# The second MLP product of an encoder block in another order of its column halves, with 48 of 64 units by seven products in place of 42

## The chip, the cores and the metric

The kernel runs on one core of one Trainium2 chip. The metric is the device time of one execution in microseconds (us), taken as the median of several runs. The engines are named as in the profile: PE is TensorE (matmul), PEld its weight load, DVE is VectorE, ACT is ScalarE, POOL is GpSimd, SP is SyncE, which issues the loads.

## The reference

One layer of an encoder: x is 256 tokens by 2048 features, in float32. Two kinds of attention with a joint output projection, a cross attention to 256 memory tokens, and an MLP, each followed by a layer norm over the residual sum.

```python
def squared_relu_mlp(h, w_mlp_in, w_mlp_out):
    return jnp.square(jax.nn.relu(h @ w_mlp_in)) @ w_mlp_out
...
        x = layer_norm(ALPHA * x + xa, ln2_g[l], ln2_b[l])

        ff = squared_relu_mlp(x, w_mlp_in[l], w_mlp_out[l])
        x = layer_norm(ALPHA * x + ff, ln3_g[l], ln3_b[l])
```

The hidden layer is 8192 wide: w_mlp_in is 2048 x 8192 and w_mlp_out 8192 x 2048. The change concerns `h @ w_mlp_out` alone.

## The kernel before, in words

**Three matmuls for one product.** Each float32 operand is split into a high half (ACT copies it to the type fp32r) and a low half (DVE subtracts the high one from the source). `mm3` (lines 163 to 166) then issues high x high, high x low and low x high: three matmuls, 128 x 128 by 128 x 512 at most. The second is the first to need the low half of the weights. ACT works ahead of DVE, and both ahead of PE, as far as four buffers for high halves (`wsp`) and four for low halves (`fixed`) let them.

**The hidden layer** has 64 tiles of 128 columns, in four chunks c of 16 (`CH`, `NCH`). One tile (`hidden_tile`, line 1021) takes a 1 MB load of w_mlp_in in two parts of 1024 columns, each split, and issues 32 matmuls: 16 of 512 columns and 16 of 256. The tile is then evacuated by one small ACT and one small DVE operation (`evacuate`, lines 870 and 871). Two tiles make a pair p. A pair passes through `stages` (line 877): relu and square on ACT (883, 884), the split into halves (874, 875), and, for a pair that a seven-product unit will use, three additions on DVE (894 to 898) and one more split. The eight tiles of the first half chunk (`LEAD`) are made ahead of the passes, in two groups (`hidden_group`).

**The second product** goes in passes (c, q): chunk c by column half q (1024 of 2048 columns), eight passes in all, numbered 0 to 7 here. A pass has eight units, one for each pair. One unit is a 2 x 2 by 2 x 2 block product: two blocks of tokens, two tiles of the pair, two groups of 512 columns, and one 1 MB load of w_mlp_out.

- A *plain* unit makes eight block products, 24 matmuls; its weights come in two parts of 1024 columns to split.
- A *seven* makes seven block products (Strassen's scheme), 21 matmuls. It needs sums of the pair's tiles (above) and sums of the weights, which DVE adds into `s_t` (`push_sums`, line 942: one addition of 1024 columns and two of 512). Its weights come in four parts: 1024 and 512 from the load, 1024 and 1024 from `s_t`.

Before, units 0 to 5 of a pass are sevens and units 6 and 7 plain, and pass 7 has eight plain units: 42 sevens and 22 plain units. Pairs 0 to 5 of each chunk get sums.

**Banks.** The eight accumulators of PSUM are four for x11, x12, x21, x22 (`xs`) and four for the products p1, p5, p6, p7 (`pt`). At the end of each pass but the last DVE merges them into the residual `res`: four additions for `xs` and eight, called `banks`, for `pt` (lines 1105 to 1111 and 1147 to 1150), behind one ACT copy of p1. The eight are taken up one or two at a time, behind the splits that follow. A hidden tile borrows x22 among the sevens, and p1 and p6 in turn elsewhere.

**The order of the work.** `items` (lines 908 to 916) is the list of tiles (g) and units (u): about one tile ahead of each unit, so that the tiles of the next half chunk are made beside the units of this one; pass 7 has none. `fetch` issues the loads on SP, three to four items ahead, into a ring of buffers that `row_b` joins at the item `JOIN`. `part` (line 958) makes one split, counts it, and behind it issues what is due: deferred work (`after(n, ...)` means n parts from now), one merge, one weight addition. `queue` fixes the order of the instructions given to it, on each engine, as they are written; other instructions (the stages of most pairs, the merges) are placed by a scheduler. The stages of tile 15's pair are queued and are written behind the unit that follows the tile (`late_finish`). Hidden pairs lie in nine slots: eight in `ht`, one in `aux`, whose other seven places hold sums. A slot is given back behind the second pass of its chunk.

**Around the passes.** The residual also needs the gain and bias of the second layer norm, in two halves of 1024 features (`norm_ops`, line 1206): four DVE operations each on `row_b`. The first half goes beside the hidden groups, the second is put into pass 1 by `after(6 * i + 8, x)`. In the last pass the last four units (`HELD`) make the products of the first block of tokens as their weights come (12 matmuls each) and keep the split weights; those of the second block follow in the end, so that the last layer norm of the first block lies beside them.

## Time and profile before

| | before |
|---|---|
| median of 3 runs | 1100.84 us (1099.25 to 1100.96) |
| profiled execution, its own time | 1098.48 us |
| span of that execution | 1096.7 us |
| PE busy | 1077.8 us, 98% of the span |
| DVE busy | 937.5 us, 85% |
| ACT busy | 638.7 us, 58% |
| granted clock of TensorE | 0.997 |

A row of a timeline has the start, the duration, the engine, the line, the operation, output and inputs and the count; in brackets stands how long the engine idled before it and who released it. The page models the ends of matmuls, so a busy PE is not PE at its peak: whether it waited is read from the distance between starts, in the same kind of work. DVE's durations overlap the next start by some 0.08 us, so costs on DVE are also read from start to start. "att" and "acc" are the two groups of four accumulators.

### The profile page before, as it was taken

Reading aid. Unit: us, or ns where it says so; the run is one execution under the profiler, and the core shown is the slowest. Engines: PE = TensorE matmul, PEld = TensorE weight load, DVE = VectorE, ACT = ScalarE, POOL = GpSimd, SP = SyncE. Lnnn points to the kernel's source line nnn. Section 1 sums busy time; section 2 is a strip of 40 time slices with the busy share of each in tenths; the row PEclk is TensorE's granted clock in tenths of the full one; section 3 lists DMA queues with packets and bytes.
Section 4 is the critical chain, followed back from the end, with each engine's and each line's share of the span. In section 5 each row is a group of like instructions: output and inputs, shape, how many; then the busy total and the mean of one; then the engine's idle time right before and its main releaser. Section 6 shows DMA issues by size and latency. Waiting matters only on the chain.

```text
span 1096.7 us, 15276 instructions
## 1 busy us (share of the span) xinstructions
PE 1077.8 (98%) x5864; PEld 931.1 (85%) x5864; DVE 937.5 (85%) x1299; ACT 638.7 (58%) x925; POOL 35.6 (3%) x45
## 2 busy tenths in 40 slices
PE   9999999999999999999999999999999999999996
PEld 6988899988999878878888888888888888888885
DVE  6878677678879677999999999899999899999876
ACT  6555566546576426656567557466566566666640
POOL 2402000000100000000000000000000000000000
PEclk9999999999999999999999999999999999999998
DMA  9663453466576444555556555646556555645732
GB/s 330 242 226 138 153 193 136 160 244 221 185 224 240 151 149 174 212 192 194 193 198 242 210 179 209 213 171 228 195 189 223 200 192 195 226 171 194 254 149 78
DMA packets 37369, 215.87 MB, mean 197 GB/s; under 512 B 4272, under 2 KB 5168, under 8 KB 13616
## 3 DMA queue, kind: packets, MB, share of 16 engines
q1 hardware_dynamic: 37296, 214.89, 55.1%
q8 instruction: 46, 0.75, 0.3%
q14 instruction: 27, 0.22, 0.1%
HBM read 212.78 MB, written 2.10 MB: 196 GB/s over the span
## 4 chain that ended last, share of the span: by engine, by line
PE 92%; DVE 6%; issue 1%; ACT 1%; DMA 0%; POOL 0%; DVEq 0%; SPq 0%; ACTq 0%
PE acc L164 12%; PE acc L165 12%; PE acc L166 12%; PE acc L1029 11%; PE att L1029 6%; PE acc L1037 6%; PE att L165 5%; PE att L166 5%; PE att L164 5%; PE att L1037 3%; PE acc L206 2%; PE acc L204 2%; PE acc L205 2%; DVE lo L956 2%; PE acc L213 1%; PE att L213 1%
## 5 line engine op out<-in xcount | busy, mean ns | idle before, releaser
L88 DVE TENSOR_TENSOR w_lo<-raw,w_hi 128x1024 fp32r<-128x1024 f32 (+2 forms) x130 | 147.4, 1142 | 60.2 <-ACT w_hi L87 59.2
L87 ACT ACTIVATE w_hi<-raw 128x1024 fp32r<-128x1024 f32 (+2 forms) x134 | 131.6, 989 | 113.9 <-PE acc L166 68.3
L956 DVE TENSOR_TENSOR lo<-raw,w_hi 128x1024 fp32r<-128x1024 f32 (+1 forms) x156 | 173.0, 1127 | 9.2 <-ACT w_hi L955 9.0
L955 ACT ACTIVATE w_hi<-raw 128x1024 fp32r<-128x1024 f32 (+1 forms) x156 | 149.3, 980 | 25.7 <-PE acc L166 15.4
L1029 PE MATMUL acc<-x2t,w_hi 128*128 128x512 f32 x592 | 153.4, 391 | 0.0
L1029 PEld LDWEIGHTS acc<-x2t,w_hi 128*128 128x128 f32 x592 | 108.9, 189 | 19.6
L956 DVE TENSOR_TENSOR lo<-s_t,w_hi 128x1024 fp32r<-128x1024 f32 x84 | 102.4, 1222 | 10.8 <-ACT w_hi L955 10.8
L955 ACT ACTIVATE w_hi<-s_t 128x1024 fp32r<-128x1024 f32 x84 | 88.6, 1057 | 37.3 <-PE acc L1029 17.1
L1037 PEld LDWEIGHTS acc<-x2t,lo 128*128 128x128 f32 x592 | 80.8, 190 | 5.8
L1037 PE MATMUL acc<-x2t,lo 128*128 128x256 f32 x592 | 82.5, 282 | 0.0
L1029 PE MATMUL att<-x2t,w_hi 128*128 128x512 f32 x304 | 78.4, 391 | 0.0
L165 PE MATMUL acc<-lo,ht 128*128 128x512 f32 (+1 forms) x188 | 73.0, 389 | 1.1 <-DVE lo L956 1.1
L164 PE MATMUL acc<-w_hi,ht 128*128 128x512 f32 x186 | 72.5, 390 | 0.0
L166 PE MATMUL acc<-w_hi,ht 128*128 128x512 f32 x186 | 72.5, 390 | 0.0
L166 PE MATMUL acc<-w_hi,xt 128*128 128x512 f32 (+2 forms) x192 | 69.6, 364 | 0.0
L165 PE MATMUL acc<-w_lo,xt 128*128 128x512 f32 (+2 forms) x192 | 69.5, 363 | 0.0
L870 ACT ACTIVATE tmp<-acc 128x256 f32<-128x256 f32 x41 | 15.4, 384 | 92.2 <-PE acc L1029 87.9
L164 PE MATMUL acc<-w_hi,xt 128*128 128x512 f32 (+2 forms) x192 | 66.4, 366 | 0.7 <-ACT w_hi L87 0.7
L1029 PEld LDWEIGHTS att<-x2t,w_hi 128*128 128x128 f32 x304 | 55.8, 189 | 10.0
L165 PE MATMUL att<-lo,aux 128*128 128x512 f32 x139 | 54.4, 392 | 1.4 <-DVE lo L956 1.4
L956 DVE TENSOR_TENSOR lo<-raw_x,w_hi 128x1024 fp32r<-128x1024 f32 (+1 forms) x50 | 55.4, 1124 | 0.3 <-ACT w_hi L955 0.2
L164 PE MATMUL att<-w_hi,aux 128*128 128x512 f32 x139 | 54.1, 390 | 0.0
(293 smaller groups left out, 2519.0 us busy)
## 6 DMA issues: line engine op xcount, KB each, us to landing
raw<-in_w_mo SPq DMA_DIRECT2D x39, 1024.0 KB, 4.8
raw<-in_w_mc SPq DMA_DIRECT2D x37, 1024.0 KB, 4.8
raw<-in_w_out SPq DMA_DIRECT2D x16, 1024.0 KB, 4.9
raw_x<-in_w_mo SPq DMA_DIRECT2D x14, 1024.0 KB, 4.9
raw_x<-in_w_mc SPq DMA_DIRECT2D x12, 1024.0 KB, 4.8
row_b<-in_w_mo SPq DMA_DIRECT2D x11, 1024.0 KB, 4.8
raw<-in_w_mi SPq DMA_DIRECT2D x8, 1024.0 KB, 4.9
row_b<-in_w_mc SPq DMA_DIRECT2D x7, 1024.0 KB, 4.7
```

The costliest lines, as they stand in the source:

```text
L87: pin(nc.scalar.activation(hi, src, AF.Copy), pinned)
L88: return pin(nc.vector.tensor_tensor(out=lo, in0=src, in1=f(hi), op=ALU.subtract), pinned)
L164: keep(nc.tensor.matmul(ps, ah, bh, start=start, stop=False))
L165: keep(nc.tensor.matmul(ps, ah, bl, start=False, stop=False))
L166: keep(nc.tensor.matmul(ps, al, bh, start=False, stop=stop))
L204: nc.tensor.matmul(ps, hi, xt[:, k, 0:S], start=k == 0, stop=False)
L205: nc.tensor.matmul(ps, hi, xt[:, k, S:2 * S], start=False, stop=False)
L206: nc.tensor.matmul(ps, lo, xt[:, k, 0:S], start=False, stop=k == nk - 1)
L955: queue(nc.scalar.activation(hi, src, AF.Copy))
L956: queue(nc.vector.tensor_tensor(out=lo, in0=src, in1=f(hi), op=ALU.subtract))
L1029: queue(nc.tensor.matmul(ps, hi[:, k * P:(k + 1) * P], x2t[:, k0 + k, :], start=k0 + k == 0, stop=k0 + k == KT - 1))
L1037: queue(nc.tensor.matmul(ps[:, 0:S], lo[:, k * P:(k + 1) * P], x2t[:, k0 + k, 0:S], start=False, stop=False))
```

## The change

1. *Order.* The passes go (0,0), (0,1), (1,1), (1,0), (2,0), (2,1), (3,1), (3,0): column halves 0, 1, 1, 0. Where two passes in a row have the same half (1-2, 3-4, 5-6) they make one run, and the banks are merged at its end only. Pass 0 and pass 7 are runs of their own.
2. *Units.* `UNITS` and `ORDERS` write out each pass: P for plain, S for seven. There are 48 S and 16 P. The plain units stand at the ends of runs; pass 0 ends with an S, and pass 7 goes P S P S and then the four held plain units.
3. *Tiles.* `TILES` writes out how many tiles stand ahead of each unit. Passes 0, 2, 4 and 6 have none ahead of their last unit.
4. *Sums.* The pairs that get sums are those of `SUMS`: six, seven, seven and six of the four chunks, 26 in place of 24. Pairs 0 and 1 of chunk 0 have none.
5. *Slots.* Hidden pairs have eight slots and sums eight.
6. *Banks.* x22 is merged by itself behind the plain units that open a run, since tiles borrow it after that. `tile_bank` chooses the bank of each tile. The eight merges of `pt` come in another order.
7. *Row operations.* The second half of `norm_ops` goes into pass 0, at parts 6, 8, 10 and 12. `JOIN` becomes unit 4 of pass 0. The first evacuation in pass 0 is deferred by three parts, not four.

```diff
-    SEVEN = (0, 1, 2, 3, 4, 5)
-    PASSES = [(c, q) for c in range(NCH) for q in range(2)]
-    ORDER = tuple(range(CH // 2))
-    SEVENS = {cq: SEVEN for cq in PASSES[:-1]}
-    SEVENS[PASSES[-1]] = ()
     HELD = 4
     LEAD = CH // 2
-    SLOTS = CH // 2 + 1
+    PASSES = [(c, (n + c) % 2) for c in range(NCH) for n in range(2)]
+    UNITS = ["PPSSSSSS", "PPSSSSSS", "SSSSSSSP", "PSSSSSSS", "SSSSSSSP", "PSSSSSSS", "SSSSSSPP", "PSPSPPPP"]
+    ORDERS = [(0, 1, 2, 3, 4, 5, 6, 7), (0, 1, 2, 3, 4, 5, 6, 7), (0, 1, 2, 3, 4, 5, 6, 7), (7, 0, 1, 2, 3, 4, 5, 6),
+              (0, 1, 2, 3, 4, 5, 6, 7), (7, 0, 1, 2, 3, 4, 5, 6), (0, 1, 2, 3, 4, 5, 6, 7), (7, 0, 6, 1, 2, 3, 4, 5)]
+    TILES = ["21111110", "21111111", "11111110", "21111111", "11111110", "21111111", "11111110", "00000000"]
+    SEVENS = {cq: [p for p, x in zip(o, u) if x == "S"] for cq, o, u in zip(PASSES, ORDERS, UNITS)}
+    SUMS = [set(SEVENS[c, 0] + SEVENS[c, 1]) for c in range(NCH)]
...
-    place, free = {}, {"h": list(range(SLOTS)), "s": list(range(len(SEVEN) + 1))}
+    place, free = {}, {"h": list(range(CH // 2)), "s": list(range(len(sums_h)))}
...
-        return [square, halve] + [add, halve_sums] * (p in SEVEN)
+        return [square, halve] + [add, halve_sums] * (p in SUMS[c])
...
+    tiles = [("g", c, j) for c in range(NCH) for j in range(CH)][LEAD:]
+    for (c, q), order, counts in zip(PASSES, ORDERS, TILES):
+        for p, n in zip(order, counts):
+            items += [tiles.pop(0) for _ in range(int(n))] + [("u", c, q, p)]
+    JOIN = items.index(("u", 0, 0, 4))
...
-            after(4, lambda: evacuate(ps, h, j % 2, queue))
+            after(3 if j == LEAD else 4, lambda: evacuate(ps, h, j % 2, queue))
...
+        opens = n == 0 or PASSES[n - 1][1] != q
+        closes = final or PASSES[n + 1][1] != q
...
+        def tile_bank(it):
+
+            before, later_ = items[:at[0] - 1], items[at[0]:]
+            units = [x for x in before if x[0] == "u"][-1:] + [x for x in later_ if x[0] == "u"][:1]
+            if all(is_seven(x) for x in units) or it[1:] == (0, LEAD):
+                return x22
+            ahead = later_[:next(i for i, x in enumerate(later_) if is_seven(x))]
+            return p1 if sum(x[0] == "g" for x in ahead) % 2 or n == len(PASSES) - 2 else p6
...
-                if n_seven == len(sevens):
+                if run["s"] == 0:
                     nc.scalar.activation(m_t, p1, AF.Copy)
+                    xs_done = [lambda r=r, ps=ps: merge(r, ps) for r, ps in ((r12, x12), (r11, x11), (r21, x21))]
+                    banks.extend([lambda: merge(r11, m_t), lambda: more(p6)] + xs_done * (units[-1] == "S") + [
+                        lambda: merge(r22, p5), lambda: merge(r12, p5),
+                        lambda: merge(r12, m_t, ALU.subtract), lambda: more(p7, ALU.subtract),
+                        lambda: merge(r21, m_t), lambda: merge(r22, m_t, ALU.subtract)])
...
+                if not final and n_unit < len(units) and units[n_unit] == "S":
+                    banks.append(lambda: merge(r22, x22))
...
-            side.extend(wait * 4 + empty + [a1, b1, a3, a2, a4, b3] + both(b2, rows[0])
-                        + both(b4, rows[1]) + rows[2:])
+            (a1, a2), (b1, b2) = first, second
+            side.extend(wait * 4 + empty + [a1, b1, a2, b2] + rows)
...
-    for cq in PASSES:
-        if cq == (0, 1):
-            for i, x in enumerate(norm_ops(1)):
-                after(6 * i + 8, x)
-        one_pass(*cq)
+    for i, x in enumerate(norm_ops(1)):
+        after(2 * i + 6, x)
+    for n in range(len(PASSES)):
+        one_pass(n)
```

## The prediction, made before the changed kernel ran

> **What bounds the kernel now.** I read the page first, then the busy time in chosen stretches, then the timelines of single engines. The page:

> ```profile
> span 1096.7 us, 15276 instructions
> PE 1077.8 (98%) x5864; PEld 931.1 (85%) x5864; DVE 937.5 (85%) x1299; ACT 638.7 (58%) x925; POOL 35.6 (3%) x45
> DVE  6878677678879677999999999899999899999876
> PE 92%; DVE 6%; issue 1%; ACT 1%; DMA 0%; POOL 0%; DVEq 0%; SPq 0%; ACTq 0%
> ```

> TensorE carries 92% of the chain that ended last. VectorE carries 6%, but from the middle of the span on it is over 90% busy: a second engine close behind the first. So I cut the MLP at the starts of hidden tiles; one stretch is a tile and the unit behind it (columns: length, then busy time of PE, PEld, DVE, ACT, POOL, then clock, DMA, GB/s).

> ```profile
> 462.53:474.04 11.51, 10.95 (x54) 8.70 (x53) 11.41 (x17) 8.21 (x12) 0.00 (x0) 1.00 0.49 169
> 474.04:485.29 11.25, 10.64 (x55) 8.78 (x53) 11.15 (x16) 6.57 (x10) 0.00 (x0) 1.00 0.54 201
> 485.29:498.03 12.74, 10.91 (x55) 8.70 (x53) 11.57 (x16) 8.92 (x12) 0.00 (x0) 1.00 0.48 166
> 498.03:508.37 10.34, 10.34 (x54) 8.86 (x53) 9.43 (x11) 6.27 (x9) 0.00 (x0) 1.00 0.57 203
> 555.88:566.70 10.82, 10.70 (x54) 8.77 (x53) 10.82 (x16) 7.49 (x11) 0.00 (x0) 1.00 0.56 194
> 566.70:577.63 10.93, 10.62 (x54) 8.78 (x53) 10.90 (x13) 6.43 (x9) 0.00 (x0) 1.00 0.56 189
> 577.63:588.91 11.28, 10.67 (x55) 8.73 (x53) 11.28 (x16) 7.48 (x11) 0.00 (x0) 1.00 0.74 269
> 599.25:610.28 11.03, 11.03 (x57) 9.42 (x56) 11.03 (x16) 6.46 (x9) 0.00 (x0) 1.00 0.65 211
> 894.40:904.75 10.35, 10.35 (x55) 8.86 (x53) 10.35 (x16) 7.33 (x10) 0.00 (x0) 1.00 0.58 204
> 904.75:915.09 10.34, 10.34 (x54) 8.86 (x53) 10.01 (x12) 6.34 (x9) 0.00 (x0) 1.00 0.57 204
> ```

> A tile with a seven-product unit takes 10.345 us where nothing waits, a tile with a plain unit 11.03 us. In six stretches, three in pass 0 and three in pass 1, it takes longer, and there DVE is busy nearly throughout. Over 10.345 us they lose 1.165 + 0.905 + 2.395 = 4.465 us in pass 0 and 0.475 + 0.585 + 0.935 = 1.995 us in pass 1: 6.46 us. One such wait, in PE's timeline:

> ```profile
> 493.68 0.50 PE L165 MATMUL acc<-lo,ht 128*128 128x512 f32 x1 [1.06 <-DVE lo L956]
> ```

> The second matmul of a group needs the low half of the weights, which DVE makes last. So the MLP is bound by TensorE's issue, except where DVE has more than 10.345 us to do in a stretch.

> **TensorE's part.** Plain minus seven is 11.03 - 10.345 = 0.685 us, three matmuls of 0.228 us. Six more sevens (42 to 48, by the strings: 6+6+7+7+7+7+6+2) remove 18 matmuls: **-4.1 us**, all on the path. The number of tiles stays. [...]

> **VectorE's part.** One cycle without a wait:

> ```profile
> 904.69 1.22 DVE L948 TENSOR_TENSOR s_t<-raw 128x1024 f32<-128x1024 f32 x1
> 905.82 1.22 DVE L956 TENSOR_TENSOR lo<-row_b,w_hi 128x1024 fp32r<-128x1024 f32 x1
> 906.96 1.41 DVE L948 TENSOR_TENSOR s_t<-s_t,raw 128x512 f32<-128x512 f32 x2
> 908.28 1.82 DVE L956 TENSOR_TENSOR lo<-raw,w_hi 128x1024 fp32r<-128x1024 f32 x2
> 910.02 1.22 DVE L956 TENSOR_TENSOR lo<-s_t,w_hi 128x1024 fp32r<-128x1024 f32 x1
> 911.16 0.42 DVE L871 TENSOR_TENSOR tmp<-acc,tmp 128x256 f32<-128x256 f32 x1
> 911.88 1.23 DVE L956 TENSOR_TENSOR lo<-s_t,w_hi 128x1024 fp32r<-128x1024 f32 x1 [0.30 <-ACT w_hi L955]
> 913.02 1.22 DVE L956 TENSOR_TENSOR lo<-raw_x,w_hi 128x1024 fp32r<-128x1024 f32 x1
> ```

> From start to start a 1024-column operation costs 1.135 us, a 512-column one 0.60 (1.74 - 1.135), two dependent adds 1.32, an evacuation about 0.36. Tile and seven: 6 x 1.135 + 0.60 + 1.32 + 0.36 = 9.1 us. Every second tile also closes a pair:

> ```profile
> 455.51 0.42 DVE L894 TENSOR_TENSOR tmp<-tmp 128x256 f32<-128x256 f32 x1
> 455.96 0.29 DVE L897 TENSOR_TENSOR tmp<-tmp 128x128 f32<-128x128 f32 x1
> 456.29 0.29 DVE L898 TENSOR_TENSOR tmp<-tmp 128x128 f32<-128x128 f32 x1
> 456.50 0.69 DVE L875 TENSOR_TENSOR ht<-tmp,ht 128x512 fp32r<-128x512 f32 x1
> ```

> That is 0.99 us of sums and two splits of 0.60: 2.2 us with sums, 0.6 without. Two cycles hold 2 x 9.1 + 2.2 = 20.4 us of DVE work in 20.69 us, as the last two stretches show (10.35 + 10.01 busy). So 13 or 14 sevens in a row (passes 1-2, 3-4, 5-6) just fit; I take no wait there. A tile with a plain unit holds 4 x 1.135 + 0.36 = 4.9 us.

> Bank merges fall from 84 to 59 (four run ends with 12 or 13 instead of seven with 12, eight in the last pass). At 0.685 us each by the grouped row below that is about 17 us less of DVE; six more sevens add 6 x 4.2 = 25 and two more pairs with sums 3.2. All of it lies beside matmuls, and the cover is the 4.9 us of DVE work beside 11 us at a run's plain ends: counted as nothing. Were that cover gone, two or three merges ahead of a run's first seven would cost 0.6 us each.

> ```profile
> L1108 DVE TENSOR_TENSOR res<-res,m_t 128x512 f32<-128x512 f32 x20 | 13.3, 685 | 0.0
> ```

> **What stalls go.** The four row operations of the second norm half (line 1209, 1024 columns each) leave pass 1; they move to the four parts 6, 8, 10 and 12 of pass 0, beside plain units with 11 us for 4.9 us of DVE. Pass 1's 1.995 us go. Pass 0's 4.465 us go too: its first two units are plain (8.2 us less DVE), and pairs 0 and 1 lose their sums (3.2 us less). **-6.46 us.** Moving JOIN to unit 4 of pass 0 puts that load behind the fourth row operation on SP's queue, still three items ahead of its use; nothing on the page's chain waits for DMA: nothing.

> **What is late next.** (1) Pass 0, fourth unit (S3). The deferred stages of pair 4 (parts 17, 18) and pair 5 (17 to 20) now fall into one cycle. Let T be PE's start of S2. From the rows, S2 behind the tile of 904.75 starts 21 x 0.228 = 4.8 us before 915.09, at 910.3, and its last split ends at 913.02: T + 2.7. DVE then does in order evacuation 3.1, split 4.2, pair 4 sums 5.2, halve 5.8, add 6.95, split 8.1, pair 4's sum split 8.7, two adds 10.0, S3's first split 11.15, needed at T + 4.8 + 5.55 + 0.23 = 10.58: late by 0.57. Pair 5 sums and halve and S3's second split end at 13.3, needed at 12.5: 0.8. Sum split and third split end at 15.05, needed at 14.0: 1.05. The fourth is in time. **+2.4 us**; between nothing (the stretch at 498.03) and the old 4.465.

> (2) The last unit of pass 0 (S7) stands right behind S6, with no tile between, and needs pair 7, whose second tile ends as S6 starts. ACT behind a tile, and then the chain of a pair 7 in the pass before the last, where that tile is followed by a plain unit:

> ```profile
> 910.79 1.05 ACT L955 ACTIVATE w_hi<-s_t 128x1024 fp32r<-128x1024 f32 x1
> 911.89 2.01 ACT L955 ACTIVATE w_hi<-raw_x 128x1024 fp32r<-128x1024 f32 x2
> 913.81 0.61 ACT L883 ACTIVATE tmp<-tmp 128x512 f32<-128x512 f32 x1
> ...
> 1032.15 0.63 ACT L883 ACTIVATE tmp<-tmp 128x512 f32<-128x512 f32 x1 [0.49 <-DVE tmp L871]
> 1032.81 0.63 ACT L884 ACTIVATE tmp<-tmp 128x512 f32<-128x512 f32 x1
> 1033.47 0.63 ACT L874 ACTIVATE ht<-tmp 128x512 fp32r<-128x512 f32 x1
> 1034.14 0.69 DVE L875 TENSOR_TENSOR ht<-tmp,ht 128x512 fp32r<-128x512 f32 x1 [2.03 <-ACT ht L874]
> ```

> With T the start of S6 (910.3 in these rows): S6's last high half ends at T + 1.5, behind it ACT starts the three steps, 0.66 us apart, at 1.5, 2.15 and 2.8; DVE's split ends at 4.1, sums 5.1, sum split 6.4. All are queued in written order, and S7's weight adds (1.135 + 1.32) come behind them: 8.85; then S7's first split: 9.95. PE needs it at 4.8 + 0.23 = 5.0. **+4.9 us** in one piece; queued behind it on DVE is every further split of S7. Low end 1.3: adds and split alone, 2.7 + 2.45 + 1.135 = 6.3. High end 6, if the merges slip in too.

> (3) In passes 2 and 4 the plain unit 7 follows such an S6: its first split ends at 4.1 + 1.135 = 5.25, needed at 5.0: 0.25 each, **+0.5** (0 to 0.5). In the last pass two sevens alternate with plain units, which hold 2.27 us of DVE work in 24 x 0.228 = 5.46 us and so leave room; then eight merges fall into the held units, which hold 2.27 us of splits in 12 x 0.228 = 2.74 us. At one merge to two splits **+0.3**; all ahead, 2.7.

> **The sum.** -4.1 - 6.46 + 2.4 + 4.9 + 0.5 + 0.3 = -2.5 us. The profiled execution took 1098.48 us (span 1096.7 and 1.8 around it), 2.4 below the median of 1100.84; 1098.48 becomes 1096.0, and the median 1098.4.

> **The rivals.** *The new waits don't come.* If the scheduler or the shorter queue keeps S7's wait to 1.3 us and the others to nothing, all of the gain stays: 1100.84 - 10.57 + 1.3 = 1091.6. For it: plain units before S2 leave DVE idle. Against: only four weight buffers let it run ahead, and the pair chain alone ends after S7's start.

> *Eight slots for hidden pairs, not nine.* Slower. In passes 1, 3 and 5 the first new pair takes the slot that the plain unit in front of it frees, so ACT's high half of that pair waits for PE to end that unit. If it stands on ACT ahead of the next tile's first split, PE waits for a 0.6 us and a 1.05 us activation, about 1.65 us, three times: 1098.4 + 5.0 = 1103.4. It decides if that activation is placed before the split rather than after. Against: at 913.81 such a stage, not ordered by hand, stands behind the next tile's two splits (911.89).

> *The clock falls in the 4.9 us wait.* After the last matmul (1086.0) the clock halves:

> ```profile
> 1086.00:1091.00 5.00, 0.00 (x0) 0.00 (x0) 4.89 (x10) 0.00 (x0) 0.92 (x1) 0.99 0.13 52
> 1091.00:1096.70 5.70, 0.00 (x0) 0.00 (x0) 1.95 (x5) 0.00 (x0) 0.00 (x0) 0.50 0.38 139
> 7.17 0.63 PE L165 MATMUL acc<-w_lo,xt 128*128 128x512 f32 x1
> 7.60 0.63 PE L166 MATMUL acc<-w_hi,xt 128*128 128x512 f32 x1
> ```

> About 4.9 us without a matmul is enough there. At half clock, as at 7.17, a matmul takes 0.43 us; S7's 21 would cost 21 x 0.2 = 4.2 us more: 1102.6. [...]

> That there are not 48 sevens is ruled out by the strings.

> **How the numbers follow.** About 0.2% (2.2 us: 1098.6 and 1103.0) is what a measurement here can tell from no change. Forecast 0.48, its own range 1096 to 1101; no new waits 0.28 (1091.6 to 1096); slots 0.13; clock 0.06; something not seen 0.05. Faster: 0.26 of the forecast and all 0.28: 0.54. Slower: 0.09 of the slots, 0.01 of the clock, 0.04 unseen: 0.14. Same: 0.32. For eight in ten the range runs from 1092.5 (a quarter of the no-wait case left out) to 1102.8 (most of the slots case left out).

> **What would show it.** In the changed profile: 18 fewer 512-column matmuls in the second product; stretches of 10.345 us in the former long places of pass 1; one PE wait of 4 to 5 us on DVE's low half behind two sevens without a tile, near 530 us; 2 to 3 us at the fourth unit of pass 0; nothing in the runs of 13 and 14. Wrong if S7's wait is under 2 us, if waits recur within the long runs, or if PE waits on ACT behind the first plain unit of passes 1, 3 and 5.

## The result and the profile after

The changed kernel takes 1107.98 us (1103.2 to 1109.19, six runs), the kernel before beside it 1100.84 us (1099.25 to 1101.14, six runs): 1.0065 times as long, 95% interval 1.0055 to 1.0076. It is slower by 7.1 us, where the prediction said 2.4 us faster; 1107.98 lies above the range.

The profiled execution took 1108.33 us. From its page: the span, the engines, and TensorE's granted clock in 40 slices.

```profile
span 1106.5 us, 15289 instructions
...
PE 1080.5 (98%) x5846; PEld 931.6 (84%) x5846; DVE 948.7 (86%) x1312; ACT 649.3 (59%) x937; POOL 38.3 (3%) x45
...
PEclk9999999999999999999899999999999999999998
```

There are 18 matmuls fewer (5846 against 5864), and yet the page calls PE busier: 1080.5 us against 1077.8. That is the first hint. Matmuls that are fewer and busier are slower, and PEclk has an 8 in its twentieth slice, in the middle of the work. Then the busy time in chosen stretches, with the columns as in the prediction:

```profile
487.05:499.99 12.94, 11.20 (x54) 8.62 (x53) 12.87 (x19) 8.90 (x12) 0.00 (x0) 1.00 0.44 163
526.25:543.14 16.89, 12.08 (x43) 9.24 (x42) 15.14 (x21) 11.11 (x14) 0.00 (x0) 0.80 0.38 146
581.13:591.47 10.34, 10.34 (x54) 8.86 (x53) 10.34 (x16) 7.32 (x10) 0.00 (x0) 1.00 0.58 203
700.51:714.44 13.93, 12.33 (x46) 9.49 (x45) 11.65 (x15) 8.46 (x11) 0.00 (x0) 0.88 0.59 225
871.17:885.10 13.93, 12.33 (x47) 9.50 (x46) 11.66 (x15) 8.46 (x11) 0.00 (x0) 0.88 0.57 216
```

The first row is a tile and the fourth unit of pass 0 (S3): 12.94 us in place of 10.34, 2.60 lost. The second is the last two units of pass 0 (S6 and S7), 42 matmuls that need 9.58 us at 0.228: 7.3 lost. The third is one of the cycles of pass 1, where the old kernel lost time: nothing is lost any more, with DVE busy throughout. The fourth and fifth are the last two units of passes 2 and 4, a seven and the plain unit 7, 45 matmuls that need 10.26 us: 3.67 lost in each, at a mean clock of 0.88. Seen from the prediction these are the surprise.

The same work ahead of the passes also came later. The first tile of pass 0 starts at 446.60 us before and at 449.06 after:

```profile
446.60 1.75 PE L1029 MATMUL acc<-x2t,w_hi 128*128 128x512 f32 x7
```
```profile
449.06 1.30 PE L1022 MATMUL acc<-x2t,w_hi 128*128 128x512 f32 x5
```

Of these 2.46 us, 1.6 are a stretch at half clock from 400.75 us on, in code that the change leaves alone; the rest is there before time 395. Together: -4.1 - 6.46 + 2.6 + 7.3 + 2 x 3.67 + 0.3 for the longer tail + 2.46 = +9.4 us of the 9.8 by which the two spans differ.

**Where unit 7 of pass 2 waits.** From the timelines of DVE and PE:

```profile
702.07 1.23 DVE L952 TENSOR_TENSOR lo<-s_t,w_hi 128x1024 fp32r<-128x1024 f32 x1 [0.52 <-ACT w_hi L951]
703.21 0.68 DVE L1108 SCALAR_TENSOR_TENSOR res<-res,m_t 128x512 f32<-128x512 f32 x1
703.82 0.68 DVE L1109 TENSOR_TENSOR res<-res,att 128x512 f32<-128x512 f32 x1
704.41 0.68 DVE L1108 SCALAR_TENSOR_TENSOR res<-res,att 128x512 f32<-128x512 f32 x1
705.01 0.68 DVE L1112 TENSOR_TENSOR m_t<-m_t,att 128x512 f32<-128x512 f32 x1
705.61 0.69 DVE L875 TENSOR_TENSOR ht<-tmp,ht 128x512 fp32r<-128x512 f32 x1
706.21 2.35 DVE L952 TENSOR_TENSOR lo<-raw,w_hi 128x1024 fp32r<-128x1024 f32 x2
...
707.49 0.50 PE L165 MATMUL acc<-lo,ht 128*128 128x512 f32 x1 [1.60 <-DVE lo L952]
708.13 0.63 PE L164 MATMUL acc<-w_hi,ht 128*128 128x512 f32 x1
```

Behind the last split of S6, DVE makes four merges (lines 1108, 1109, 1112), then pair 7's split (875), and only at 706.21 the first split of the plain unit. PE issues its first matmul at 705.38 and its second at 707.49: 1.88 us more than the usual step. From 708 on the matmuls follow each other at 0.43 us in place of 0.228. The clock by stretches of 3.41 us shows why:

```profile
704.54:707.95 3.41, 1.81 (x8) 1.01 (x7) 3.41 (x5) 3.41 (x4) 0.00 (x0) 1.00 0.00 0
707.95:711.36 3.41, 3.41 (x10) 2.62 (x9) 2.88 (x3) 0.21 (x1) 0.00 (x0) 0.50 0.50 154
530.46:533.87 3.41, 1.24 (x5) 0.46 (x3) 2.64 (x5) 2.10 (x3) 0.00 (x0) 1.00 0.00 0
533.87:537.28 3.41, 0.77 (x2) 0.68 (x3) 3.35 (x5) 2.11 (x2) 0.00 (x0) 0.50 0.00 0
```

In this trace the half clock lasts 3.41 us or twice that (6.83 us at S7), and its starts (400.75, 533.87, 707.95, 878.62) are 133.12, 174.08 and 170.67 us apart: 39, 51 and 50 steps of 3.413 us. The stretches above are cut at the edges of this grid. The one from 704.54, in which PE was busy 1.81 of 3.41 us by the profile, was followed by one at a granted clock of 0.50. Half of such a stretch, 1.7 us, is lost: 1.88 of wait and 1.7 to 1.8 of slow matmuls are the loss of 3.67.

**Where S7 waits.** PE and DVE:

```profile
530.81 0.39 PE L166 MATMUL acc<-w_hi,ht 128*128 128x512 f32 x1
533.01 0.50 PE L164 MATMUL att<-w_hi,ht 128*128 128x512 f32 x1 [1.81 <-ACT w_hi L951]
536.51 0.80 PE L165 MATMUL att<-lo,ht 128*128 128x512 f32 x1 [3.00 <-DVE lo L952]
...
532.04 0.69 DVE L875 TENSOR_TENSOR aux<-tmp,aux 128x512 fp32r<-128x512 f32 x1 [0.69 <-ACT aux L874]
532.65 1.22 DVE L944 TENSOR_TENSOR s_t<-row_b 128x1024 f32<-128x1024 f32 x1
533.90 1.42 DVE L944 TENSOR_TENSOR s_t<-s_t,row_b 128x512 f32<-128x512 f32 x2
535.23 1.82 DVE L952 TENSOR_TENSOR lo<-row_b,w_hi 128x1024 fp32r<-128x1024 f32 x2
```

The order is the predicted one: pair 7's sum split (532.04), then the weight additions, then S7's first split. The wait comes in two pieces, 1.97 us for the high half (ACT splits `row_b` only after pair 7's sums) and 3.27 us for the low half: 5.24 us for the predicted 4.9. What the forecast left to a rival is the rest: two stretches at a granted clock of 0.50 (533.87 to 540.70), 2.0 us.

### The profile page after: what moved, and what is told of

Same layout as the page of the kernel before. It is cut to its first block, busy times and chain, and to the rows that moved or that the text cites. A ratio compares the mean times of both kernels' runs of the same rounds, so it can differ in the third digit from the quotient of the medians.

```text
span 1106.5 us, 15289 instructions
## 1 busy us (share of the span) xinstructions
PE 1080.5 (98%) x5846; PEld 931.6 (84%) x5846; DVE 948.7 (86%) x1312; ACT 649.3 (59%) x937; POOL 38.3 (3%) x45
## 4 chain that ended last, share of the span: by engine, by line
PE 90%; DVE 6%; DMA 2%; ACT 1%; issue 1%; SPq 0%; POOL 0%; DVEq 0%; ACTq 0%
PE acc L1022 14%; PE acc L165 11%; PE acc L164 11%; PE acc L166 11%; PE acc L1030 7%; PE att L1022 5%; PE att L165 4%; PE att L166 4%; PE att L164 4%; PE att L1030 2%; PE acc L206 2%; PE acc L204 2%; PE acc L205 2%; PE acc L213 1%; PE att L213 1%; DVE lo L952 1%
## 5 line engine op out<-in xcount | busy, mean ns | idle before, releaser
L1022 PE MATMUL acc<-x2t,w_hi 128*128 128x512 f32 x672 | 174.2, 391 | 0.0
L952 DVE TENSOR_TENSOR lo<-raw,w_hi 128x1024 fp32r<-128x1024 f32 (+1 forms) x148 | 162.2, 1116 | 7.2 <-ACT w_hi L951 7.2
L1022 PEld LDWEIGHTS acc<-x2t,w_hi 128*128 128x128 f32 x672 | 123.7, 189 | 22.2
L952 DVE TENSOR_TENSOR lo<-s_t,w_hi 128x1024 fp32r<-128x1024 f32 x96 | 117.1, 1222 | 18.6 <-ACT w_hi L951 18.6
L951 ACT ACTIVATE w_hi<-s_t 128x1024 fp32r<-128x1024 f32 x96 | 101.4, 1057 | 42.7 <-DVE lo L952 18.4
L1030 PEld LDWEIGHTS acc<-x2t,lo 128*128 128x128 f32 x672 | 91.7, 190 | 6.5
L1030 PE MATMUL acc<-x2t,lo 128*128 128x256 f32 x672 | 93.7, 282 | 0.0
L165 PE MATMUL acc<-lo,ht 128*128 128x512 f32 x174 | 69.5, 400 | 3.9 <-DVE lo L952 3.9
L165 PE MATMUL acc<-w_lo,xt 128*128 128x512 f32 (+2 forms) x192 | 69.4, 363 | 0.7 <-DVE w_lo L88 0.7
L166 PE MATMUL acc<-w_hi,xt 128*128 128x512 f32 (+2 forms) x192 | 69.2, 361 | 0.0
L166 PE MATMUL acc<-w_hi,ht 128*128 128x512 f32 x174 | 69.1, 397 | 0.0
L1022 PE MATMUL att<-x2t,w_hi 128*128 128x512 f32 x224 | 57.7, 391 | 0.0
L165 PE MATMUL att<-lo,aux 128*128 128x512 f32 x140 | 54.7, 391 | 0.8 <-DVE lo L952 0.8
L164 PE MATMUL att<-w_hi,aux 128*128 128x512 f32 x140 | 54.7, 391 | 0.0
L166 PE MATMUL att<-w_hi,aux 128*128 128x512 f32 x140 | 54.5, 389 | 0.0
L952 DVE TENSOR_TENSOR lo<-raw_x,w_hi 128x1024 fp32r<-128x1024 f32 (+1 forms) x48 | 52.3, 1109 | 1.1 <-ACT w_hi L951 1.1
```

Source lines behind the costliest of these rows:

```text
L164: keep(nc.tensor.matmul(ps, ah, bh, start=start, stop=False))
L165: keep(nc.tensor.matmul(ps, ah, bl, start=False, stop=False))
L166: keep(nc.tensor.matmul(ps, al, bh, start=False, stop=stop))
L951: queue(nc.scalar.activation(hi, src, AF.Copy))
L952: queue(nc.vector.tensor_tensor(out=lo, in0=src, in1=f(hi), op=ALU.subtract))
L1022: queue(nc.tensor.matmul(ps, hi[:, k * P:(k + 1) * P], x2t[:, k0 + k, :], start=k0 + k == 0, stop=k0 + k == KT - 1))
```

## The experiments

**Theory.** Waits in and behind sevens (S3, S7, and unit 7 of passes 2 and 4) give back more than the change saves, and all but S3 also halve TensorE's clock. **Rivals:** the 48 sevens are too much for VectorE anywhere; the new order of column halves itself costs; the merges cost their time wherever they stand. Each experiment has its own runs of the kernel before beside it (medians of 1099.36 to 1100.6 us), so the experiments are compared by their ratios to it; that of the changed kernel is 1.0065.

**1. The clock alone.** Nothing is taken from any wait; matmuls on a constant, whose result nothing reads, fill PE while it waits: 20 ahead of S7, 7 ahead of unit 7 in passes 2 and 4.

```diff
+            for ps, m in {(0, 8): ((x22, 20),), (2, 8): ((p1, 7),), (4, 8): ((p1, 7),)}.get((n, n_unit), ()):
+                for _ in range(m):
+                    queue(nc.tensor.matmul(ps, ones, ones[:, None, :].broadcast_to([P, 4, P]),
+                                           start=True, stop=True))
```

> The changed kernel, with matmuls that compute nothing put into the three waits on PE: 20 ahead of the last unit of pass 0 (into the idle x22 bank), 7 ahead of unit 7 in passes 2 and 4 (into the idle p1 bank). They take away no wait, only the idleness of PE. Theory W (idleness halves the clock): the clock stays full at these three places, the waits for the low half end at the same times, 2.0 + 2 x 1.75 = 5.5 us less, 1102.5 us. Rival F (the stretches have another cause): the same number of half-clock stretches, 1108 us or a little more, because the filler itself takes PE time.

Measured: 1101.5 us (1101.07 to 1103.73), 1.0019 times the kernel before (1.001 to 1.0028). PE's timeline around S7:

```profile
528.98 4.49 PE L1133 MATMUL acc<-ones 128*128 128x512 bf16 x20
533.12 0.58 PE L164 MATMUL att<-w_hi,ht 128*128 128x512 f32 x1
534.45 0.50 PE L165 MATMUL att<-lo,ht 128*128 128x512 f32 x1 [0.75 <-DVE lo L952]
```

S7's data come as late as before (its second matmul starts 10.26 us behind the start of S6 in both traces), but the matmuls behind run at full clock (1.00 for S6 and S7, in place of 0.80), and up to the tail nothing in this trace is at half clock (mean 0.996, in place of 0.990). Useless matmuls took the ratio from 1.0065 to 1.0019, 5.1 us: most of the loss against the kernel before is the clock, and idle time of PE is what halved it at these places. The traces have the same 5.1 us at the three places filled: S6 and S7 take 14.93 us in place of 16.89, the last two units of passes 2 and 4 12.34 and 12.35 in place of 13.93.

**2. The merges behind the splits, in all passes.** Handing the eight merges of `pt` to `queue` fixes them behind the splits written ahead of them.

```diff
-                    banks.extend([lambda: merge(r11, m_t), lambda: more(p6)] + xs_done * (units[-1] == "S") + [
+                    banks.extend([lambda: queue(merge(r11, m_t)), lambda: queue(more(p6))] + xs_done * (units[-1] == "S") + [
```

(and so for the other six.)

> The changed kernel, with the eight merges of the p banks ordered as they are written, behind the splits; nothing else. Theory W (the last units of passes 2 and 4 wait because four merges stand on DVE ahead of their first split, and each such wait of about 1.9 us also halves the clock for one stretch of 3.4 us): the waits at units 7 of passes 2 and 4 fall from 1.9 to 0.7 us or less, no half-clock stretch there, about 2 x 3 us less, 1102 us. Rival F (the half-clock stretches come whatever PE waits): the waits fall by 2 x 1.2 us, the stretches stay in number, 1105.5 us. Rival D (the merges only move the wait to the next tile): no change, 1108 us.

Measured: 1109.37 us (1108.33 to 1110.41), 1.008 (1.0067 to 1.0093): a miss. The wait of unit 7 did shrink, to 1.03 us in each of passes 2 and 4, with no half clock there (the mean granted clock of this trace is 0.996, that of the changed kernel 0.990). The time went into the last pass; ACT, DVE and PE:

```profile
1068.65 0.57 ACT L1147 ACTIVATE m_t<-acc 128x512 f32<-128x512 f32 x1
...
1069.26 0.69 DVE L1109 TENSOR_TENSOR res<-res,m_t 128x512 f32<-128x512 f32 x1 [3.80 <-ACT m_t L1147]
1070.66 1.22 DVE L952 TENSOR_TENSOR aux<-raw,wide 128x1024 fp32r<-128x1024 f32 x1
...
1071.93 0.50 PE L165 MATMUL att<-aux,ht 128*128 128x512 f32 x1 [3.67 <-DVE aux L952]
```

In the held units of pass 7 ACT splits six parts ahead of its copy of p1 into `m_t` (1068.65). The first merge needs that copy; with its place fixed it stops DVE for 3.80 us, and the split that PE needs stands behind it. Where the scheduler could place the merges, it put splits ahead. With three smaller waits the last pass loses 3.83 + 0.81 + 0.96 + 0.85 = 6.45 us.

**3. The same, but only for runs that end before the last two passes.**

```diff
+                    late_q = queue if n < 6 else lambda ins: ins
-                    banks.extend([lambda: queue(merge(r11, m_t)), lambda: queue(more(p6))] + ...
+                    banks.extend([lambda: late_q(merge(r11, m_t)), lambda: late_q(more(p6))] + ...
```

> The merges of the p banks wait behind the splits of the next unit as in e1_behind, but only where they close a run that ends before the last two passes; those that close the run of pass 6, and the merges and statistics of pass 7 behind them, stay where the changed kernel has them. Theory (in e1_behind the wait ahead of passes 2 and 4's plain unit did shrink, and the gain was eaten by 3.83 + 0.81 + 0.96 + 0.85 = 6.45 us of new waits in the last pass): against the changed kernel's 1107.98 us, twice 0.85 us of wait and twice 1.8 us of halved clock go, so 1102.7 us (1101 to 1104.5), with no PE wait over 0.5 us after time 1060. Rival (the merges cost their time wherever they stand): 1107 us or more again, with the waits at another place before the last pass.

Measured: 1101.55 us (1101.11 to 1103.6), 1.0014 (1.0005 to 1.0022), 5.6 us less by the ratios. DVE, PE and ACT at the end of pass 2:

```profile
703.63 1.23 DVE L952 TENSOR_TENSOR lo<-raw,w_hi 128x1024 fp32r<-128x1024 f32 x1 [0.26 <-ACT w_hi L951]
704.77 0.68 DVE L1108 SCALAR_TENSOR_TENSOR res<-res,m_t 128x512 f32<-128x512 f32 x1
...
704.91 0.50 PE L165 MATMUL acc<-lo,ht 128*128 128x512 f32 x1 [0.77 <-DVE lo L952]
705.25 0.40 PE L166 MATMUL acc<-w_hi,ht 128*128 128x512 f32 x1
...
700.21 0.59 ACT L1147 ACTIVATE m_t<-att 128x512 f32<-128x512 f32 x1
...
702.55 1.99 ACT L951 ACTIVATE w_hi<-raw 128x1024 fp32r<-128x1024 f32 x2
```

The first split now stands ahead of the merges, the wait is 1.03 us, and the step of the next matmuls stays at 0.23. The last two units take 11.47 and 11.51 us in passes 2 and 4 in place of 13.93, 4.9 us less together. The merges have not become fewer: their place cost 0.85 us of wait, and the clock fell with it. The 1.03 us that stay have nothing to do with merges. ACT copies p1 into `m_t` first (700.21, 0.48 us from start to start), then makes the three steps of pair 7, and only at 702.55 begins with the high half of the plain unit, for which DVE idles 0.26 us at 703.63.

**4. Pair 4's stages earlier**, so that they don't meet pair 5's at S3.

```diff
-            n = 11 if j == LEAD + 1 else 5
+            n = 5
```

> The changed kernel, with the stages of pair 4 deferred by 5 parts, not 11, so that they fall beside the plain units of pass 0 and not into one cycle with those of pair 5. Theory (two pairs' stages in one cycle make the 2.6 us wait at the fourth unit of pass 0): that wait falls to 0.7 us or less, about 2 us less, 1106 us. Rival (the wait is the weight adds and the four splits of the seven alone, four buffers ahead): the wait stays at 2.6 us, 1108 us.

Measured: 1106.51 us (1105.77 to 1108.26), 1.006 (1.0046 to 1.0074): not told apart from the changed kernel. Of S3's three waits (0.39, 0.91 and 0.94 us) the first is gone, the second is longer, the third stays:

```profile
493.29 0.50 PE L165 MATMUL acc<-lo,ht 128*128 128x512 f32 x1 [1.05 <-DVE lo L952]
495.03 0.50 PE L165 MATMUL att<-lo,aux 128*128 128x512 f32 x1 [0.78 <-DVE lo L952]
```

S3 takes 7.20 us in place of 7.38: taking the two pairs apart, whose meeting the prediction named as the cause, gives back 0.2 us of 2.6. But DVE is no longer full there:

```profile
491.08 0.42 DVE L871 TENSOR_TENSOR tmp<-acc,tmp 128x256 f32<-128x256 f32 x1 [1.71 <-ACT tmp L870]
492.55 0.68 DVE L952 TENSOR_TENSOR lo<-raw_x,w_hi 128x512 fp32r<-128x512 f32 x1
```

It idles 1.71 us ahead of the evacuation of the tile just made, and S3's second split (492.55) stands behind that evacuation. In the changed kernel DVE is busy for 12.87 of the 12.94 us and has the order of the prediction; here an operation that stands too early on DVE takes the place of the load. How long S3 would take without both was not tried.

**5. The last unit of pass 0 plain**, with pair 7's additions and their split put off (47 sevens).

```diff
-    UNITS = ["PPSSSSSS", ...
+    UNITS = ["PPSSSSSP", ...
...
-                for stage in stages(h, c, j // 2, queue if j == CH - 1 else free_order):
+                todo = stages(h, c, j // 2, queue if j == CH - 1 else free_order)
+                if c == 0 and j == CH - 1:
+                    for n, stage in zip((3, 4), todo[2:]):
+                        after(n, stage)
+                    todo = todo[:2]
+                for stage in todo:
```

> The changed kernel with the last unit of pass 0 plain (47 sevens, 3 matmuls more, 0.7 us) and pair 7's addition and its split put off by three and four tiles or units; the merges stay free. Theory 1 (the 7.3 us at pass 0's last unit are the price of a seven right behind the stages of its own pair): they go, and what stays is the split of a plain unit behind four merges as in passes 2 and 4, 1.9 us with 1.75 us of halved clock: 1107.98 + 0.7 - 7.3 + 3.6 = 1105.0 us (1103.5 to 1106). Theory 2 (the merges find VectorE idle there): 1101.4 us. Rival (the wait is for the stages whatever the unit is): 1107.5 us or more.

Measured: 1103.36 us (1100.49 to 1104.84), 1.0025 (1.0017 to 1.0034): between the first theory's 1105.0, just under its bounds, and the second's 1101.4, and clear of the rival. The trace decides for the first. It shows the plain unit of pass 0 in exactly the trouble of passes 2 and 4: 1.88 us of wait in each of the three, each followed by 3.41 us at half clock. The stretches of the clock at the first:

```profile
529.18:532.59 3.41, 1.81 (x7) 1.24 (x7) 3.41 (x5) 2.87 (x4) 0.00 (x0) 1.00 0.00 0
532.59:536.00 3.41, 3.41 (x9) 2.67 (x8) 3.04 (x5) 1.12 (x2) 0.00 (x0) 0.50 0.65 247
```

**6. The same order with 42 sevens.** Only the strings are changed: passes 0 to 6 end in two plain units wherever a run closes.

```diff
-    UNITS = ["PPSSSSSS", "PPSSSSSS", "SSSSSSSP", "PSSSSSSS", "SSSSSSSP", "PSSSSSSS", "SSSSSSPP", "PSPSPPPP"]
+    UNITS = ["PPSSSSPP", "PPSSSSSS", "SSSSSSPP", "PPSSSSSS", "SSSSSSPP", "PPSSSSSS", "SSSSSSPP", "PSPSPPPP"]
```

> The changed order of column halves and tiles with 42 units by seven products instead of 48: passes 0 to 6 end in two plain units where the changed kernel ends in one or none, and passes 1, 3 and 5 begin with two. Theory A (the loss lies in where a run of sevens ends, not in the number of sevens): 18 matmuls more are 4.1 us; the 5.2 us of wait and 2 us of halved clock at pass 0's last unit go, since that unit is plain; the waits of 1.9 us with their halved clock move one unit forward in passes 2 and 4: 1107.98 + 4.1 - 7.2 = 1104.9 us (1103 to 1107). Theory B (48 sevens are too many for VectorE, the order itself is free): all waits behind time 520 go, 1107.98 + 4.1 - 7.2 - 7.3 = 1097.6 us. Rival C (the order itself costs): 1108 us or more.

Measured: 1114.46 us (1111.6 to 1114.74), 1.0122 (1.0109 to 1.0135): above theory A's 1104.9 and B's 1097.6, on the side of rival C, but not by its reason. A new wait is there, in PE's and DVE's timelines:

```profile
519.12 0.39 PE L166 MATMUL acc<-w_hi,ht 128*128 128x512 f32 x1
523.04 3.75 PE L1022 MATMUL att<-x2t,w_hi 128*128 128x512 f32 x8 [3.53 <-DVE m_t L1112]
...
522.22 0.67 DVE L1112 TENSOR_TENSOR m_t<-m_t,att 128x512 f32<-128x512 f32 x1
```

With the last seven one place further forward, a hidden tile now stands between it and the next unit, and that tile borrows p6 as its bank: its first matmul waits until DVE has merged p6 (522.22, ending at 522.89), 3.7 us, and 3.42 us in passes 2 and 4. Each is followed by slow matmuls, as at half clock: 3.75 us for the eight from 523.04 on, 2.90 us for the six from 699.43 and 3.24 us for the eight from 872.69, where a step of 0.228 us makes 2.0 us for eight and 1.5 for six. In the changed kernel no tile stands there (`TILES` ends in 0), so the run's end waits for one split and not for its banks. So 42 sevens are not better: this version sheds S7's wait and takes on a worse one. It does not tell what the order costs with 42 sevens and another place for that tile, which wasn't tried; experiments 8 and 9 say more on the order.

**7. Experiments 2, 4 and 5 together.**

> The changed kernel with the merges behind the splits, pair 4 early, and the last unit of pass 0 plain (47 sevens, not 48), the sums of pair 7 deferred behind the next pass's first tile. Theory W: the 5.2 us wait of pass 0 and the 2.0 us of half clock in it go for 0.7 us of matmuls, passes 2 and 4 give 6 us and the fourth unit 2 us: 1093 to 1095 us, faster than both kernels. Rival (the DVE work only moves on and every run end keeps a wait of 2 us with its half-clock stretch): 1102 us or more.

Measured: 1104.39 us (1103.85 to 1105.99), 1.0038 (1.0025 to 1.005): a miss, where 1093 to 1095 was expected. The last pass has the waits of experiment 2 again (3.84, 0.85 and 0.31 us), and the longest is followed by 3.41 us at half clock.

**8. Experiments 3, 4 and 5 together** (47 sevens, the last pass left as it was).

> e5_all with the same restriction: the merges wait behind the splits in passes 0 to 5 alone; pair 4's stages come early; the last unit of pass 0 is plain (47 units by seven products), pair 7's sums put off. Theory: e5_all's 1104.39 us less its waits of the last pass (3.83 + 0.85 + 0.31 us) and less the halved clock that stood at 1069 us (1.7 us): 1097.7 us (1096 to 1099), which is below the kernel before (1099.4 us on this chip). Rival (what is saved at one place is waited for at another): 1101 us or more.

Measured: 1098.28 us (1096.11 to 1099.23), 0.9976 (0.9967 to 0.9984). The first version that beats the kernel before, and near the 1097.7 us (1096 to 1099) worked out from the waits of the one before.

**9. A third plain unit at the start of pass 0** (46 sevens).

```diff
-    UNITS = ["PPSSSSSP", ...
+    UNITS = ["PPPSSSSP", ...
```

> e7_three with a third plain unit at the start of pass 0 (46 units by seven products): the unit that still waits 1.21 + 0.93 us there is plain and needs 3 matmuls more (0.7 us). Theory (the wait is for the weight additions and their splits, which a plain unit doesn't need): 1098.28 - 2.1 + 0.7 = 1096.9 us (1096 to 1098.5). Rival (VectorE is behind with pair 4 and 5's stages, and the next unit waits in its place): 1098.5 us or more, with the two waits one unit later.

Measured: 1095.33 us (1095.11 to 1097.14) beside 1100.6 us for the kernel before, 0.9961 (0.9948 to 0.9975), a little under the range expected. From the page, then DVE's and PE's timelines:

```profile
PE 1074.6 (98%) x5852; PEld 927.8 (85%) x5852; DVE 941.6 (86%) x1303; ACT 645.8 (59%) x933; POOL 38.3 (4%) x45
...
488.85 1.23 DVE L952 TENSOR_TENSOR lo<-s_t,w_hi 128x1024 fp32r<-128x1024 f32 x1 [1.55 <-ACT w_hi L951]
...
538.93 1.21 PE L1030 MATMUL att<-x2t,lo 128*128 128x256 f32 x8 [0.56 <-DVE lo L952]
```

The expectation takes the unit that becomes plain for the one that waits, but it is the unit ahead of it: S3 is still a seven, with all its weight additions and splits. Even so its waits are gone, and nothing waits in their place: its third split is made at 488.85, ahead of its first matmul at 491.31. So the theory as written was not what was tried. What held S3 up hangs on the unit ahead being a seven; whether by its load on DVE or by the place of pair 5's stages, which count the parts, stays open. What remains is 1.03 us in each of passes 0, 2 and 4 and 0.72 us in the tile at 538.93. Six matmuls more than in the changed kernel (5852 for 5846): two sevens fewer, in the right places, and the merges a few places later turn a loss of 0.65% into a gain of 0.39%. This is the fastest version of the study. Experiments 8 and 9 keep the new order and its runs of 13 and 14 sevens, and no wait shows in those runs, so neither the order as such nor the sevens of the long runs cost the time.

## Why the prediction was wrong

*The matmuls saved, -4.1 us:* right; 5846 for 5864, and cycles of 10.34 us.

*The old stalls, -6.46 us:* right. Those of pass 1 are gone, the runs of 13 and 14 sevens show no wait, and pass 0's old ones are gone too.

*S3, +2.4 us:* 2.6 measured. In the changed kernel the size and the order on DVE were right. But the meeting of two pairs is not all there is: with pair 4 moved away 2.4 us stay, with DVE idle for 1.71 us ahead of an evacuation (experiment 4). With a plain unit ahead, S3 did not wait at all (experiment 9).

*S7, +4.9 us of wait:* 5.24 measured, by the chain that was named. Its price was 7.3, since the clock fell as well.

*Passes 2 and 4, 0.25 us each:* **the step that failed.** It took for granted that the plain unit's first split stands behind pair 7's split alone, and bounded the wait by 0 and 0.5; it was 1.88. The prediction had the merges slip in only as the high end of S7, and said of all merges "counted as nothing", covered by 4.9 us of work beside 11 us. But that cover lies in a cycle of tile and plain unit. Here no tile stands, the banks come free one after the other while PE is still in the last seven, and four merges took the place ahead of the split. Experiment 3 moved only their place and took the wait to 1.03 us, so 0.85 us were the merges. The other 0.78 us above the forecast were on ACT, which the prediction left out of this sum: the copy of p1 ahead of pair 7's steps (0.48 us) and the plain unit's own high half behind them. And each wait of 1.88 us halved the clock, 1.7 to 1.8 us more. The lesson of the row at 703.21: work that is hidden on average is not hidden at the one point where a split is due, and the place of instructions that a scheduler orders has to be priced at both ends.

*The clock:* the rival was right that an idle PE costs the clock, but it was tied to the 4.9 us wait, with a chance of 0.06. The half clock came there and at both waits of 1.88 us, about 5.6 us in all. Experiment 1 shows it: filled with useless matmuls, the same late data cost 5.1 us less. The price of 0.43 us for a matmul was right too: it is the step from 708.13 on, at a granted clock of 0.50. (For the rows at 7.17, from which it was taken, the profile shows no half clock: 1.00 from 7 to 8 us.) A wait of 4.9 us was not needed: stretches with PE busy 1.81 of 3.41 us were enough in all five cases of the changed kernel and experiment 5.

*The last pass, +0.3 us:* the tail behind the last matmul is 0.3 us longer, and no PE wait shows there. *Slots:* no wait on ACT behind the first plain unit of passes 1, 3 and 5; that rival is out. *No new waits:* out.

In one sum: the forecast of -2.5 us, with 2.4 more at S7, 6.8 more at passes 2 and 4 and 0.2 at S3, gives +6.9 us; the medians differ by 7.1. The two profiled executions differ by more, 9.8 us, since that of the kernel before was 2.4 us under its median.

## What to carry to other kernels

When a tuned kernel is reordered, look at the points where runs end: what becomes free there (banks, copies, sums) rushes onto the second engine just when the first unit behind needs it, and an average of the cycle doesn't show it. Price each wait of TensorE twice, once for itself and once for the clock: here all five waits of 1.88 us, with PE busy 1.81 of 3.41 us, were followed by half clock, which cost 1.7 to 1.8 us more. A wait that can't be removed can be filled, which took the ratio from 1.0065 to 1.0019. And fix the order of a stray instruction only where all that it needs is there in time: the same line took the ratio from 1.0065 to 1.0014 with six passes, and to 1.008 with eight.

## What the runs showed of the hardware

```profile
1066.76:1070.17 3.41, 1.50 (x7) 0.92 (x5) 0.81 (x2) 3.41 (x6) 0.00 (x0) 1.00 0.39 161
1070.17:1073.59 3.42, 1.66 (x6) 1.05 (x6) 3.42 (x5) 0.95 (x2) 0.00 (x0) 1.00 0.00 0
...
1066.05:1069.46 3.41, 0.39 (x2) 0.35 (x3) 2.96 (x4) 2.21 (x3) 0.00 (x0) 1.00 0.00 0
1069.46:1072.88 3.42, 3.42 (x10) 2.40 (x9) 3.38 (x6) 0.00 (x0) 0.00 (x0) 0.50 0.00 0
```

How idle a stretch has to be stays open. PE was busy for 1.81 us or less, by the profile, in every stretch read here that was followed by half clock; but the two of experiment 2, with 1.50 and 1.66 us, were not followed by it, nor was one with 1.77 us (from 527.45). The profile models the ends of matmuls, and the grid's edges are known only by the changes of clock. Behind a wait of 1.03 us the granted clock stayed at 1.00: in passes 2 and 4 of experiment 3 (PE busy 2.65 of 3.41 us) and in pass 0 of experiment 9 (2.67).

The same idle place was followed by half clock in some executions only. Near 400 us, ahead of all that the change touches, PE was busy for 5.72 or 5.73 us of the 8 from 396 to 404, in the kernel before, the changed kernel and experiments 1, 5, 8 and 9 alike. The clock halved there in the changed kernel (from 400.75 us) and in experiments 7 and 8 (from 400.45 and 399.74 us); it stayed at 1.00 from 400 to 404 us in the kernel before and in experiments 1, 5 and 9. What the clock does to the times of one program is not shown, as one execution of each kernel has a trace: one run of the changed kernel took 1103.2 us at a mean clock of 0.995, the others 1106.8 to 1109.2 at 0.990 or 0.991.
